# A 4096-cube matmul with GELU: two groups of output blocks pass from one level of Strassen to two, and the first group is planned anew

## The chip, the core and the metric

The kernel runs on one core of a Trainium2 chip. The metric is the device time of one execution in microseconds (us). The profile names the engines PE (TensorE, matmuls), PEld (its weight loads), DVE (VectorE), ACT (ScalarE), POOL (GpSimd) and SP (SyncE). POOL and SP do no arithmetic here: each issues DMAs, in the order in which they stand in its own queue, and sixteen DMA engines carry them out. The kernel before takes 1444.3 us in the median of three runs (1443.88 to 1444.35).

## The reference

```python
m, k, n = 4096, 4096, 4096            # a: m x k, b: k x n, both float32
x = np.matmul(a, b)
out = 0.5 * x * (1 + np.tanh(np.sqrt(2 / np.pi) * (x + 0.044715 * x**3)))   # float32
```

## The kernel before

**Blocks.** A, B and the output are each cut into four quadrants of 2048 x 2048. Rows of A are taken in four rows of blocks (mb 0 to 3; each has 512 rows of the upper and 512 of the lower half), columns of B in four blocks (nb 0 to 3; 512 columns of the left and 512 of the right half). One row of A against one block of B is a *group*: 16 groups, each 1024 x 1024 of the output over the whole inner size 4096. Plainly done, a group is 512 matmuls of 128 x 128 weights by 512 columns.

**One level of Strassen.** In Winograd's form a group is seven products P1 to P7 of sums of quadrants, 64 matmuls each: 448. Operands are float16. B is cast from float32 on its way in (a POOL DMA); A is cast in the same way into a staging buffer and turned by DVE (STREAM_TRANSPOSE). DVE makes the sums of quadrants (`combine2`, L956).

**Three kinds of group.** The list `groups` (mb, nb) orders them: row 0 takes B's blocks 0 1 2 3, row 1 takes 3 0 1 2, row 2 takes 2 3 0 1, row 3 takes 1 2 3 0.

- Group 0 (`first_group`, L782) is written out by hand: the first half of the inner size plainly (L633), the second half by Strassen (L589), 480 matmuls, so that work can start before all quadrants are there.
- Groups 1 to 5 are *raw groups* (`raw_group`, L1502): quadrants of B are loaded, their sums made in place and used at once (L589), and those sums that later groups need are stored to DRAM as *units* (`k_unit`, 512 KB each, by SP). Some of their products are cut once more (`RAW_CUT`): one cut product is 110 matmuls of 256 columns (L1041) and two of 512 in place of 64.
- Groups 6 to 15 are taken in pairs (`late_pair`, L1765): two blocks of B stand side by side for one row of A, and each of P1 to P7 is done by a second level of Strassen, in fourteen steps (`ORDER`) of 8 matmuls of 512 columns (L1864): 112 a product, 784 a pair. Units come back from DRAM (POOL), or B's quadrants are cast again from the input, for the units named in `FROM_INPUT`; `cast_unit` casts from DRAM to DRAM, so that a later pair can fetch. Sums between the four accumulators of each half are moved by ACT copies (L1873, L1876) and DVE adds (L1314, L1319).

`PARK` names pairs that put eight partial sums in DRAM and read them again. When a row of A ends, `turn_quad` loads the next row's four quadrants. Each block's squares (`square`, ACT) and each row's (`weigh`) are summed, for a check of the numbers' range at the end.

**What sets the order.** From group 1 on nothing is issued when it is written: each step is put in a `Plan` with its dependencies, and `schedule` (L235) orders each engine's queue by due times and by tables of costs (`COST`, `MOVE`, `WEIGHT`); `CHOICE` and `EARLIER` are hand-set exceptions. The result is a fixed order on each engine; on the chip only semaphores decide when each step starts.

## Time and profile before

| | us |
|---|---|
| median of the runs (3) | 1444.3 |
| the profiled execution: span from first to last instruction | 1444.0 |
| PE busy | 1434.2 |
| DVE busy | 1224.2 |
| ACT busy | 706.2 |
| groups 4 and 5 (matmuls of the two raw groups) | from 402.0 to 591.3 |
| the five pairs | from 591.3 to 1438.2 |

The span is the time of one core from its first to its last instruction. A busy engine has an instruction running; the DMA issues of POOL and SP are not counted. The share of the DMA engines adds up the time of packets, which overlap: it goes over 1 (1.34 where nothing but casts runs), so it does not by itself say how much more the engines could carry. The granted TensorE clock is 1.00 throughout.

### The profile page before, as it was taken

What the parts mean: (1) busy time and instruction counts of PE and PEld (TensorE: products, weight loads), DVE (VectorE), ACT (ScalarE), POOL (GpSimd) and SP (SyncE); (2) the same over time, 40 slices, a digit from 0 to 9 for tenths busy, and PEclk for the clock granted to TensorE, in tenths of its full rate; (3) what the DMA queues carried; (4) which work ended last, traced back from release to release, by engine and by line L of the source; (5) the groups of instructions that cost most, each with busy time, mean ns of one, the idle gap of its engine ahead of it and who ended that gap; (6) DMA issues with size and microseconds to landing.
All of it is one profiled execution on the core that took longest, in us unless ns stands there. A gap on an engine that the chain in (4) does not pass through costs nothing.

```text
span 1444.0 us, 20205 instructions
## 1 busy us (share of the span) xinstructions
PE 1434.2 (99%) x7011; PEld 686.1 (48%) x7011; DVE 1224.2 (85%) x1335; ACT 706.2 (49%) x1484; POOL 484.8 (34%) x888
## 2 busy tenths in 40 slices
PE   9999999999999999999999999999999999999998
PEld 3444464564545646444444444444444444444443
DVE  2598988996879999989998999888997998968776
ACT  5656764465885453463645413462564612433133
POOL 8765251343244513332322343221323212211120
PEclk9999999999999999999999999999999999999999
DMA  9999999999999999998979999979899966875773
GB/s 170 198 221 240 299 268 267 258 269 263 241 240 244 242 307 248 269 299 280 315 268 324 260 326 316 315 228 322 235 342 248 323 225 226 301 253 209 264 255 119
DMA packets 205181, 378.94 MB, mean 262 GB/s; under 512 B 21008, under 2 KB 115728, under 8 KB 205072
## 3 DMA queue, kind: packets, MB, share of 16 engines
q0 software_dynamic: 146752, 245.42, 70.5%
q1 hardware_dynamic: 58320, 132.15, 24.3%
q8 instruction: 57, 0.93, 0.2%
q14 instruction: 52, 0.43, 0.1%
HBM read 333.45 MB, written 138.42 MB: 327 GB/s over the span
## 4 chain that ended last, share of the span: by engine, by line
PE 93%; DMA 3%; POOL 1%; DVE 1%; issue 1%; ACT 0%; DVEq 0%; ACTq 0%; POOLq 0%
PE acc L1864 56%; PE acc L589 29%; PE acc L1041 6%; PE acc L633 2%; DMA stage<-in_a_dram 2%; DMA out_dram<-y 1%; POOL bR L493 1%; POOL stage L493 1%; DMA bR<-k_unit 1%; DMA bR<-in_b_dram 0%; DVE bR L956 0%; DVE stage L956 0%; ACT y L1292 0%; DVE y L1314 0%; DVE acc L1319 0%
## 5 line engine op out<-in xcount | busy, mean ns | idle before, releaser
L1864 PE MATMUL acc<-bR 128*128 128x512 f16 x1536 | 339.5, 379 | 0.1
L956 DVE TENSOR_TENSOR bR<-bR 128x2048 f16<-128x2048 f16 (+1 forms) x163 | 268.0, 1658 | 41.0 <-PE acc L1864 27.7
L1864 PEld LDWEIGHTS <-bR 128*128 128x128 f16 x1776 | 173.8, 98 | 209.9 <-issue 0.4
L830 POOL DMA_DIRECT2D bR<-k_unit x234 | 126.6, 543 | 434.0 <-PE acc L1864 318.0
L589 PE MATMUL acc<-bR,aT 128*128 128x512 f16 x1024 | 226.2, 379 | 0.0
L1864 PE MATMUL acc<-bR,aT 128*128 128x512 f16 x1008 | 223.6, 379 | 0.0
L830 POOL DMA_DIRECT2D bR<-in_b_dram x256 | 138.0, 545 | 221.2 <-DVE bR L956 69.3
L1864 PEld LDWEIGHTS <-aT 128*128 128x128 f16 x1344 | 131.5, 98 | 158.6
L1876 ACT COPY acc<-acc 128x512 f32<-128x512 f32 x140 | 79.8, 570 | 227.6 <-PE acc L1864 213.2
L1314 DVE TENSOR_TENSOR y<-acc,y 128x512 f32<-128x512 f32 x253 | 167.0, 682 | 21.3 <-ACT y L1308 9.8
L589 PE MATMUL acc<-bR,aD 128*128 128x512 f16 x832 | 180.9, 379 | 0.0
L589 PEld LDWEIGHTS <-aT 128*128 128x128 f16 x1088 | 106.5, 98 | 123.0
L1394 ACT ACTIVATE y<-bR 128x1024 bf16<-128x1024 f16 x128 | 130.8, 1052 | 55.1 <-DVE y L1399 53.4
L589 PEld LDWEIGHTS <-aD 128*128 128x128 f16 x928 | 90.6, 98 | 110.0 <-DVE aD L574 0.8
L1292 ACT ACTIVATE y<-y 128x512 f32<-128x512 f32 x158 | 97.4, 629 | 87.7 <-DVE y L1314 87.3
L1864 PE MATMUL acc<-bR,aD 128*128 128x512 f16 x624 | 138.4, 379 | 0.3 <-DVE bR L956 0.3
L1864 PEld LDWEIGHTS <-aD 128*128 128x128 f16 x784 | 76.6, 98 | 93.1 <-DVE bR L956 0.8
L1873 ACT COPY y<-acc 128x512 f32<-128x512 f32 x99 | 58.0, 586 | 99.4 <-PE acc L1864 85.9
L1399 DVE TENSOR_TENSOR y<-y 128x1024 bf16<-128x1024 bf16 x120 | 82.0, 685 | 17.4 <-ACT y L1394 16.1
L466 DVE STREAM_TRANSPOSE aT<-stage 128x1024 uint32<-128x1024 uint32 (+2 forms) x42 | 52.5, 1277 | 34.9 <-DMA stage<-in_a_dram 32.1
L1864 PE MATMUL acc<-stage,aT 128*128 128x512 f16 x336 | 75.6, 379 | 0.0
L1319 DVE TENSOR_TENSOR acc<-acc,y 128x512 f32<-128x512 f32 x100 | 67.9, 691 | 4.3 <-ACT y L1873 3.0
(126 smaller groups left out, 1682.0 us busy)
## 6 DMA issues: line engine op xcount, KB each, us to landing
bR<-k_unit POOLq DMA_DIRECT2D x234, 512.0 KB, 7.6
out_dram<-y SPq DMA_DIRECT2D x198, 256.0 KB, 7.2
bR<-in_b_dram POOLq DMA_DIRECT2D x352, 128.0 KB, 6.2
k_unit<-bR SPq DMA_DIRECT2D x76, 512.0 KB, 6.0
stage<-in_a_dram POOLq DMA_DIRECT2D x92, 256.0 KB, 10.1
stage<-k_unit POOLq DMA_DIRECT2D x46, 512.0 KB, 7.8
k_unit<-stage SPq DMA_DIRECT2D x28, 512.0 KB, 5.6
out_dram<-bR SPq DMA_DIRECT2D x46, 256.0 KB, 8.2
```

The source lines that it names most:

```text
L589: nc.tensor.matmul(acc, sa[:, j // 2, i * P : (i + 1) * P, j % 2], sb[:, j, :], start=start and j == 0, stop=stop and j == 3, skip_group_c ...
L830: return plan.add(queue, COST[queue], lambda: eng.dma_start(out=dst, in_=src), r=r, w=w, size=MOVE[what] * SPREAD, weight=weight, **kw)
L956: nc.vector.tensor_tensor(out=dst, in0=xa, in1=ya, op=ALU.add if op > 0 else ALU.subtract)
L1041: nc.tensor.matmul(PS[s][i][:, :] if wide else PS[s][i][:, w * HC : (w + 1) * HC], sa[:, j // 2, r * P : (r + 1) * P, j % 2], rhs(j, wide) ...
L1292: act("gelu", lambda: nc.scalar.activation(t, t, ACT.Gelu_apprx_tanh), [("f", f)], [("f", f)])
L1314: dve("add", lambda: nc.vector.tensor_tensor(out=sm(g), in0=bank(s, i), in1=sm(f), op=ALU.add), [("f", f)], [("f", g), ("p", s, i)])
L1319: dve("add", lambda: nc.vector.tensor_tensor(out=bank(s, i), in0=bank(s, i), in1=sm(f), op=ALU.add), [("f", f)], [("p", s, i)])
L1394: act("square", lambda t=t, src=src: nc.scalar.activation(t, src, ACT.Square), [c(cx)], [("f", f)], slack=60.0)
L1399: dve("add16", lambda t=t, u=u: nc.vector.tensor_tensor(out=u, in0=u, in1=t, op=ALU.add), [("f", f)], [("f", e)], slack=60.0)
L1864: nc.tensor.matmul(bank(w, i), sa[:, jx // 2, r * P : (r + 1) * P, jx % 2], bv[:, jx, :], start=p in "17" and jx == 0, stop=jx == NJ - 1, ...
L1873: act("copy", lambda: nc.scalar.copy(out=sm(f), in_=bank(w, i)), [("p", w, i)], [("f", f)])
L1876: act("copy", lambda: nc.scalar.copy(out=bank(*dst), in_=bank(*x)), [("p", *x)], [("p", *dst)])
```

## The change

Groups 4 and 5 become a sixth pair. Row 0 of A is done by group 0 and three raw groups (1, 2, 3), and rows 1, 2 and 3 wholly by pairs; the order of B's blocks in the rows is now written out (`ROWS`), row 1 beginning with the pair of blocks 1 and 2. The raw groups' extra cuts go with the two groups, so that four of seven remain. Row 1 of A is loaded by `turn_quad` at the end of group 3, and must be there for the first pair. The first pair isn't parked.

Group 0 keeps its 480 matmuls but is written into the plan (after two plain steps). It now also stores block 0's sums P4 to P7 (16 units), which before were stored when block 0 was loaded a second time in group 5; and the squares of three of its quadrants' first halves are taken by DVE, not ACT. Buffers are dealt out differently, the planner's costs, due times and exceptions have new values, and `FROM_INPUT` and `CASTS` name other units.

Over the whole program the instructions that the change removes and adds are these:

| | before | after |
|---|---|---|
| PE: matmuls of 512 columns / of 256 | 6241 / 770 | 6315 / 440 |
| DVE: sums of 128x4096 | 107 | 133 |
| DVE: sums of 2048 columns (all forms) | 402 | 356 |
| DVE: adds of 128x512 | 559 | 591 |
| DVE: adds, sums and squares of 1024 columns | 124 | 132 |
| DVE: turns of 1024 / of 2048 | 57 / 3 | 63 / 0 |
| DVE: adds of 128x256 | 30 | 18 |
| ACT: copies of 128x512 / of 128x256 | 396 / 56 | 440 / 32 |
| ACT: squares of 128x1024 | 128 | 116 |
| POOL: casts of B, 128 KB | 416 | 464 |
| POOL: casts of A, 128 KB / 256 KB | 40 / 108 | 8 / 124 |
| POOL: fetches of a unit, 512 KB | 280 | 304 |
| POOL and SP: parked sums, 256 KB, out and back | 40 and 40 | 32 and 32 |
| SP: stores of a unit, 512 KB | 104 | 98 |

Three places show how the queues change. First PE, where group 3 ends. Before, the last rows of group 3's cut product (L1041) are followed by group 4, the next raw group (L589, acc is the accumulator, bR a buffer of B, aT a turned quadrant of A, aD a sum):

```order
L1041 LDWEIGHTS aD
L1041 MATMUL acc<-bR,aD 128x256
L589 LDWEIGHTS aT
L589 MATMUL acc<-bR,aT 128x512
```

Now the same rows of group 3 (L837) are followed by the first pair (L1653), whose B lies in what was the staging buffer:

```order
L837 LDWEIGHTS aD
L837 MATMUL acc<-bR,aD 128x256
L1653 LDWEIGHTS aT
L1653 MATMUL acc<-stage,aT 128x512
```

So the pairs begin two raw groups earlier in PE's list. Second POOL, which issues the loads for this place. Before, the casts of A's row 1 stand among fetches and the long run of casts for blocks 3, 0 and the units:

```order
L830 DMA bR<-in_b_dram 32x4x512 x146
L830 DMA stage<-in_a_dram 32x8x512 x8
L830 DMA bR<-in_b_dram 32x4x512 x14
L830 DMA stage<-in_a_dram 32x8x512 x8
L830 DMA bR<-k_unit 128x2048 x4
```

Now, with the first pair's P1 and P2 of block 1 cast from the input and block 2's fetched, these loads and A's row 1 stand close together:

```order
L630 DMA bR<-in_b_dram 32x4x512 x5
L630 DMA stage<-k_unit 128x2048
L630 DMA bR<-in_b_dram 32x4x512 x3
L630 DMA stage<-k_unit 128x2048
L630 DMA bR<-in_a_dram 32x8x512 x4
L630 DMA bR<-in_b_dram 32x4x512 x3
L630 DMA bR<-in_a_dram 32x8x512 x4
L630 DMA bR<-in_b_dram 32x4x512 x2
L630 DMA bR<-k_unit 128x2048 x2
L630 DMA bR<-in_b_dram 32x4x512 x8
```

The last row holds the second half of block 1's P2, for the fifth step of the first pair's second product. Third SP, at the start of its queue. Before, it begins with group 0's sixteen outputs:

```order
L696 DMA out_dram<-y 128x512 x12
L696 DMA out_dram<-aD 128x512 x4
L830 DMA k_unit<-bR 128x2048 x3
L830 DMA out_dram<-y 128x512
L830 DMA k_unit<-bR 128x2048
```

Now block 0's stores come ahead of and between them:

```order
L630 DMA k_unit<-bR 128x2048 x2
L630 DMA k_unit<-aD 128x2048 x2
L630 DMA k_unit<-bR 128x2048 x2
L630 DMA out_dram<-y 128x512
L630 DMA k_unit<-bR 128x2048 x4
L630 DMA out_dram<-y 128x512 x10
```

Ten stores of 512 KB thus stand ahead of all but one of group 0's outputs.

The diff, cut to its core (new names with a trailing underscore are helpers of the new `first_group`):

```diff
-BUSY = {"PE": 13.0, "DVE": 15.5, "ACT": 18.0, "POOL": 10.4, "SP": 15.5}
+BUSY = {"PE": 20.2, "DVE": 15.3, "ACT": 20.4, "POOL": 12.2, "SP": 5.0}
...
-N_RAW = 6
+CHOICE = {}
+EARLIER = {}
+N_RAW = 4
 RAW_MAKES = {}
-RAW_CUT = {1: "P3", 2: "P7 P3", 3: "P3", 4: "P7 P3", 5: "P7"}
+RAW_CUT = {1: "P3", 2: "P7 P3", 3: "P3"}
 GROUPS = {
+    4: modes_of(m="P1 P2 P3 P4 P5 P6 P7"),
+    5: modes_of(m="P1 P2 P3 P4 P5 P6 P7"),
...
+SQ = {"12": True, "11": True, "22": False, "21": True}
+ROWS = ((0, 1, 2, 3), (1, 2, 3, 0), (3, 0, 1, 2), (3, 2, 1, 0))
...
-FROM_INPUT = ((0, "P2"), (1, "P1"), (1, "P2"), (1, "P3"), (2, "P3"), (3, "P3"))
+FROM_INPUT = ((0, 'P1'), (0, 'P2'), (0, 'P3'), (1, 'P3'), (1, 'P1'), (1, 'P2'), (3, 'P3'))
+STORE_AT = {}
...
-CASTS = {4: ((1, 'P3'), (2, 'P3')), (8, 'P5'): ((0, 'P2'),)}
+CASTS = {(8, 'P5'): ((1, 'P3'), (1, 'P1')), (4, 'P5'): ((0, 'P3'),), (4, 'P6'): ((0, 'P1'),), (4, 'P2'): ((0, 'P2'),)}
...
-PARK = (6, 8, 10, 12, 14)
+PARK = (8, 10, 12, 14)
...
-CHANGED_A = (2, 3)
-CHANGED_B = {(nb, name) for nb, pairs in ((0, (10, 14)), (2, (6, 8, 12))) for name in NAMES
+CHANGED_A = (1, 2, 3)
+CHANGED_B = {(nb, name) for nb, pairs in ((0, (4, 10, 14)), (2, (6, 8, 12))) for name in NAMES
...
+    def first_group():
+        X, Y = 0, 1
...
+        load_b_("11", 0)
+        load_a_("21", 0)
+        plain_pe("11", "11", "11", X, True)
+        square(b_slot["12"], 0, "12", range(4), SQ["12"])
+        square(b_slot["11"], 0, "11", range(4), SQ["11"])
+        load_a_("12", 0)
+        load_b_("22", 0)
...
+        gate = load_a_("12", 1)[-1:]
...
+        keep_t("P7", S["12"][lo], (0, 1), gate, EARLY_STORE)
+        for i in half_pe(X, lambda q: a_quarter(raw("11"), q), S["11"][hi], True):
+            add_bank(xs[i], X, i)
...
+        first = load_raw(1, "11", slots["b"]["11"])
+        send(3, first[-1:])
...
-        first_group()
-        load_raw(1, "12", slots["b"]["12"])
-        behind[1, "P2"] = load_raw(1, "22", slots["b"]["22"])
-        first_weights()
+        first_steps()
+        ends = first_group()
+        pending = raw_group(1, NAMES, RAW_MAKES.get(1, ()), next_nb=2, ends=ends)
+        pending = raw_group(2, NAMES, RAW_MAKES.get(2, ()), next_nb=3, pending=pending)
+        raw_group(3, NAMES, (), turn=1, pending=pending)
         free_cells.extend(ST)
-        pending = raw_group(1, NAMES, RAW_MAKES.get(1, ()), next_nb=2)
-        pending = raw_group(2, NAMES, RAW_MAKES.get(2, ()), next_nb=3, pending=pending)
-        raw_group(3, ("P1", "P2", "P5"), (), turn=1, pending=pending)
-        free_cells.extend(ST)
-        pending = raw_group(4, ("P3", "P4", "P6", "P7"), RAW_MAKES.get(4, ()), fetch=("P5", "P7"), next_nb=0)
-        raw_group(5, NAMES, RAW_MAKES.get(5, ()), pending=pending)
```

More of the change, by code (lines that the diff above doesn't have):

```diff
@@ L764, in half_path @@
+    before = {}
+    for n, whats in ((0, "A11_0a B12_0a A11_0b B12_0b T11_0a T11_0r T11_0s W11_0"),):
+        for what in whats.split():
+            half = what[-1] == "0" and what != "A11_0"
             if what[0] == "W":
-                xs = range(*(int(x) for x in what[6:].split("-"))) if what[6:] else range(NX)
-                before.setdefault(n, []).append((weigh_first, (what[1:3], int(what[4]), xs)))
+                before.setdefault(n, []).append((weigh_first, (what[1:3], int(what[4]), range(NX))))
@@ L1379, in cast_unit, with spare, square @@
                 dma("POOL", dst, src, [], toks, "raw_b", batch=("cu", nb, name, cc), slack=CAST_SLACK, after=after)
-    def square(slot, nb, quad):
+        on_hand.add((nb, name))
+    def spare(nb):
+        energy["n"] += 1
+        return SPARES[nb][energy["n"] % len(SPARES[nb])]
+    def square(slot, nb, quad, xs=range(8), by_dve=False, lead=0.0):
         half = quad[1]
-        for x in range(8):
+        for x in xs:
             cx = slot * 4 + x // 2
@@ L1657, in p4_ends @@
             if turn:
-                turn_quad(turn, "22", raw("22"), (24, 26))
-            if next_nb is None and gi + 1 in REFETCH:
-                for q in range(QPH):
-                    fetch_unit_to(nb, "P2", q, s21[q])
+                turn_quad(turn, "22", raw("22"), (ST[0], ST[2]))
+            if next_nb is None:
+                free_cells.extend(s21)
         def third():
-            return stages_of(split(Y, blk(s2), made_beside(s22) if turn else here(s22), True), c12)
+            return stages_of(split(Y, blk(s2), here(s22), True), c12)
         later_, after = None, lambda: load_next("22", "22")
@@ L1755, in whole_pair @@
                         fetch_unit_to(nb, name, q, cells[q])
-        for nb in nbs:
-            first_use.difference_update({(nb, name, cc) for cc in range(CH)})
+        on_hand.update((nb, name) for nb in nbs if STORE_AT.get((nb, name)) == ga)
         fetched_by[name] = [o for o in plan.ops[begun:] if o.eng == "POOL"]
```

620 lines of the change are left out of this document (288 added, 332 removed).

## The prediction

> **What bounds the kernel now.** I read the page's busy times and chain first, then what PE waited for, then the chain in order of time, and last the stretches and the DMA queues. The page says that PE is the bound:
>
> ```profile
> PE 1434.2 (99%) x7011; PEld 686.1 (48%) x7011; DVE 1224.2 (85%) x1335; ACT 706.2 (49%) x1484; POOL 484.8 (34%) x888
> PE 93%; DMA 3%; POOL 1%; DVE 1%; issue 1%; ACT 0%; DVEq 0%; ACTq 0%; POOLq 0%
> ```
>
> What PE waited for, all told (us, times, longest):
>
> ```profile
> PE acc L633 <- DVE aT L466: 1.7, 1, 1.7
> PE acc L598 <- DVE table L785: 1.5, 1, 1.5
> PE acc L1864 <- DVE bR L956: 0.3, 1, 0.3
> PE acc L589 <- DVE aD L574: 0.3, 1, 0.3
> ```
>
> Once under way PE loses 0.6 us in the whole run. So work taken from PE is time gained, as long as what feeds it keeps up, and there the cover is thinner: DVE is 85% busy, and the DMA engines carry most of the time. Two views price both sides. The chain in order of time (start, us, what) gives PE's rates and the edges of the groups:
>
> ```profile
> 3.42 4.95 DMA stage<-in_a_dram
> 14.78 26.20 PE acc L633 x120
> 195.37 3.49 PE acc L1041 x32
> 402.02 58.71 PE acc L589 x272
> 591.28 355.71 PE acc L1864 x1648
> ```
>
> A matmul of 512 columns takes 355.71 / 1648 = 0.2158 us, one of 256 columns 3.49 / 32 = 0.1091. Groups 4 and 5 run from 402.02 to 591.28. The first loads move at 3.4 us. The timeline of PE at the start and at the end:
>
> ```profile
> 11.14 1.89 PE L633 MATMUL acc<-bR,aT 128*128 128x512 f16 x8
> 1434.54 3.62 PE L1864 MATMUL acc<-bR,aT 128*128 128x512 f16 x16
> ```
>
> PE does eight real matmuls, stops, and goes on at 14.78 with 8 x 0.2158 = 1.7 us done: from there it runs 14.78 - 1.7 = 13.1 us behind its own work. I call this the lead: a load may be 13.1 us late against PE's count of work before it stops PE again. The last matmul ends at 1438.2, and 5.8 us of last adds and stores follow, which the change leaves.
>
> The stretches (PE, PEld, DVE, ACT, POOL busy, clock, DMA share, GB/s landed), and the DMA queues of three of them in the same order (packets, MB, share):
>
> ```profile
> 10.00:80.00 70.00, 68.25 (x317) 30.61 (x315) 33.10 (x36) 44.35 (x193) 53.79 (x96) 1.00 1.34 198
> 90.00:230.00 140.00, 140.00 (x704) 68.78 (x703) 126.81 (x154) 90.75 (x171) 65.86 (x123) 1.00 1.13 264
> 150.00:156.00 6.00, 6.00 (x30) 2.73 (x28) 6.00 (x7) 3.69 (x11) 0.00 (x0) 1.00 1.04 417
> 591.00:760.00 169.00, 169.00 (x785) 76.62 (x784) 156.80 (x158) 84.96 (x193) 51.33 (x94) 1.00 0.95 286
> ```
>
> ```profile
> q0 software_dynamic: 21628, 13.76, 133.8%
> ...
> q0 software_dynamic: 18360, 16.62, 74.0%
> q1 hardware_dynamic: 7846, 20.21, 38.6%
> ...
> q1 hardware_dynamic: 884, 2.50, 103.9%
> ```
>
> From 10 to 80 us only casts move: 198 GB/s, so 128 KB (131,072 bytes) cost 0.662 us of all sixteen engines. From 150 to 156 only stores move: 417 GB/s, so 512 KB cost 1.257 us and a 256 KB output 0.629. From 90 to 230 both are mixed, and these prices explain 16.62 MB / 198 + 20.21 MB / 417 = 83.9 + 48.5 = 132.4 of 140 us, or 0.946, pauses in it counted as loss. So the engines are all but full there already. The granted clock is 1.00 in every row, and nothing here changes it.
>
> **The change part by part.** *PE.* The two raw groups take 591.28 - 402.02 = 189.3 us; the pair in their place is 784 x 0.2158 = 169.2. By counts it is the same: 330 matmuls of 256 columns go, 74 of 512 come, 16.0 - 36.0 = -20.0 us. Group 0 keeps its 480 matmuls. **-20.0 us**, all on the path.
>
> *DVE, ACT, POOL.* Prices by form (busy, mean ns), with one row of ACT and one of POOL behind them:
>
> ```profile
> L1314 DVE TENSOR_TENSOR y<-acc,y 128x512 f32<-128x512 f32 x253 | 167.0, 682 | 21.3 <-ACT y L1308 9.8 <-PE acc L1864 6.8 <-PE acc L1041 2.0
> L956 DVE TENSOR_TENSOR bR<-bR 128x4096 f16<-128x4096 f16 x67 | 153.0, 2287 | 33.0 <-PE acc L1864 27.7 <-DMA bR<-k_unit 5.1
> L956 DVE TENSOR_TENSOR bR<-bR 128x2048 f16<-128x2048 f16 x96 | 115.1, 1218 | 8.0 <-PE acc L589 5.7 <-DMA bR<-in_b_dram 0.9 <-PE acc L1041 0.7
> L1399 DVE TENSOR_TENSOR y<-y 128x1024 bf16<-128x1024 bf16 x120 | 82.0, 685 | 17.4 <-ACT y L1394 16.1
> L466 DVE STREAM_TRANSPOSE aT<-stage 128x1024 uint32<-128x1024 uint32 x37 | 44.2, 1225 | 29.4 <-DMA stage<-in_a_dram 26.5 <-ACT y L607 1.5 <-ACT stage L502 1.3
> ...
> L1876 ACT COPY acc<-acc 128x512 f32<-128x512 f32 x140 | 79.8, 570 | 227.6 <-PE acc L1864 213.2 <-DVE y L1314 14.0
> ...
> L830 POOL DMA_DIRECT2D bR<-in_b_dram x256 | 138.0, 545 | 221.2 <-DVE bR L956 69.3 <-DMA bR<-in_b_dram 41.9 <-PE acc L589 41.3
> ```
>
> 26 x 2.287 - 46 x 1.218 + 32 x 0.682 + 8 x 0.685 + 6 x 1.225 less three long turns of 2.3 and twelve short adds of 0.4 gives 59.5 - 56.0 + 21.8 + 5.5 + 7.4 - 11.7 = +26 us: 1250 of some 1424, 88% for 85%. A pair already runs with DVE at 156.80 / 169 = 93% and PE does not wait, so I cost it at **0**; the cover is that DVE works ahead, and the rival below prices its end. *ACT*: 44 copies more at 0.57, 24 short ones and 12 squares fewer, +4 us at 49% busy: 0. *POOL*: 48 more issues of 0.55 us at 34% busy: 0 for itself; what its queue holds up is the next term, since a cast that waits for a buffer stops all behind it. *Tail*: the last pair is as before, 0.
>
> *The DMA engines up to the first pair.* This is the step that matters: the pair comes 189 us earlier, and its operands with it. Count the queues down to the last row of the POOL piece shown above, the second half of block 1's P2. POOL has by then 288 casts of B of 128 KB, and of A 8 of 128 KB and 60 of 256 KB: 288 + 8 + 120 = 416 units of 128 KB, 416 x 0.662 = 275.4 us. Six fetches, at the store's price: 7.5. SP has by then the 84 stores of blocks 0 to 3 (105.6) and the 64 outputs of row 0 (40.3), whose buffers the pair takes over. The sum is **428.8 us**. Moving from 3.4 us on without a pause it is done at 432.2. PE's work before that step is 480 + 1096 matmuls of 512 and 440 of 256 for group 0 and three raw groups, and 112 + 32 of the pair: 1720 x 0.2158 + 440 x 0.1091 = 419.2 us; with the lead of 13.1 it stands there at 432.3. So with perfect engines the load lands just as PE comes, and each per cent that they lose after the casts of the first 80 us (76.6 us of the 428.8) costs PE 3.5 us. At the mixed stretch's 0.946 the other 352.2 take 372.3, and the stall is 20 us; at 1.00 it is 0. The truth lies between: 0.946 holds pauses in which the queues of before had nothing to send, while the queues now are never empty so early. I take the middle, 0.973: 362.0, a stall of 9.8, and with a us from landing to use **+11 us** (0 to 21). Two earlier places are as tight: at the first sum of A's second half, 104 units of 128 KB at 68.8 + 3.4, a turn (1.2) and a sum (1.2) meet PE at 62.2 + 13.1 with 0.7 us to spare, and at group 1's third quarter 192 units, 15 stores and 18 outputs (157.3 us) leave 3 us before PE, at 152.0. Each can stop PE for a us; I put **+1**.
>
> Over the run the DMA engines get 48 more casts (31.8 us), 24 more fetches (30.2), and lose 6 stores and 16 moves of parked sums (17.6): +44 us, most of it early. After the first pair the later pairs have the load that the row of 591 to 760 shows, 169 us in which PE lost nothing.
>
> **The sum**, against the profiled execution's 1444.0: 1444.0 - 20.0 + 11 + 1 = **1436 us**. The median of the runs is 0.3 above that execution, which I leave out.
>
> A rule weighed against these rows: the Trainium skill, DMA: Bandwidth & Descriptors, section Bandwidth, has the memory's side bind transfers between HBM and SBUF at about 358 GB/s for a core. The casts' row speaks against it, since 198 GB/s landed in float16 are 396 read in float32. What the rule would make of the pinch is the last rival.
>
> **The rivals.** *The engines keep up.* Backlogged queues lose next to nothing, and PE meets each load as it lands: 1424 to 1428. For it: the casts' 70 us, without a pause. Against it: the mixed row's 0.946. *The mixed stream loses more.* Casts wait in POOL's queue for buffers that DVE and PE free, and the stall reaches 17 to 23 us in all (no change) at 0.959 to 0.944, and more below that: at 0.92 it is 32, and the time 1456. From 0.944 down this is slower than before; the row of 90 to 230 stands at that edge. *DVE becomes the bound.* It was idle for 1444.0 - 1224.2 = 219.8 us; if it can shed none of that, the span is 1250 + 220 = 1470, and it is slower unless 23 us of it go. Part is forced, as where it waits for PE's accumulators:
>
> ```profile
> DVE bR L956 <- PE acc L1864: 67.6, 69, 2.9
> DVE aT L466 <- DMA stage<-in_a_dram: 32.1, 10, 9.2
> ```
>
> Against it: the first are a us each, and the longest of the second, 9.2 us, is in the first loads, where DVE now has squares to do. *A ceiling on bytes.* If what is read and written in memory counted, the 416 casts read 109 MB, and fetches, stores and outputs are 64 MB more; were these held to the 382 GB/s that the row of 90 to 230 shows by the same count (2 x 16.62 + 20.21 MB in 140 us), 173 MB end at 456, a stall of 24 and the two us of above, and 1450. By the page's 358 they would take 483 us, and the time be some 1478; the casts' row excludes that figure, not the mechanism. *That the change doesn't do what it says* is excluded by the counts of PE's list.
>
> **How the numbers follow.** Changes under 0.2% (2.9 us) can't be told from none here. My forecast, a stall of 4 to 17 us (1428 to 1441), has 0.48; the engines keeping up 0.18; the mixed stream losing more 0.21, of which 0.10 falls within 0.2%; DVE 0.09 (0.03 within); the ceiling 0.04 (slower). So faster 0.66, same 0.13, slower 0.21. The range leaves out half of the second case and the worst of the last three: 1426 to 1455; the likeliest case's own is 1428 to 1441.
>
> **What would show it.** Right: PE's matmuls busy some 20 us less; its waits name DMA loads of bR, some 10 us, in the steps of the first pair near 400 to 435 us, and nearly none after; stretches up to there have the DMA engines full at 260 GB/s or more. Wrong: waits of PE on DVE's sums spread over the pairs (DVE), waits already in group 0 or in groups 1 to 3 (mixed stream), or no wait at all.

## The result and the profile after

The changed kernel takes **1477.2 us** (median; 1474.5 to 1479.7) against 1444.3: a ratio of **1.0229** (95% interval 1.021 to 1.0248), slower by 33 us. The prediction was 1436, range 1426 to 1455. The profiled execution has a span of 1475.6 us, 31.6 above the one of before.

The page after, its busy line and its chain:

```profile
PE 1426.0 (97%) x6755; PEld 661.7 (45%) x6755; DVE 1260.0 (85%) x1346; ACT 716.9 (49%) x1492; POOL 512.1 (35%) x936
...
PE 42%; DVE 0%; ACT 0%; issue 0%
```

PE has 256 matmuls fewer, as counted, but is busy only 8.2 us less, not 20.0, and idle for 1475.6 - 1426.0 = 49.6 us where it was idle for 9.8. The chain reaches back 42% of the span on PE alone, then breaks up. So, between the two profiled executions: -20.0 of work, +11.8 of matmuls that run slower, +39.8 of idle time, together 31.6.

The view of PE's waits (us, times, longest) names DVE's sums first, but it only says who came last:

```profile
PE acc L1653 <- DVE bR L756: 11.3, 7, 4.8
PE acc L537 <- DVE stage L756: 10.6, 3, 7.0
PE acc L537 <- DVE aD L756: 5.1, 1, 5.1
```

The stretches after (PE, PEld, DVE, ACT, POOL busy, granted clock, DMA share, GB/s):

```profile
10.00:100.00 90.00, 80.34 (x361) 35.22 (x360) 68.42 (x87) 78.33 (x267) 54.19 (x95) 0.98 1.30 208
100.00:190.00 90.00, 81.33 (x364) 36.09 (x363) 71.50 (x86) 51.61 (x82) 34.53 (x64) 0.96 1.10 281
190.00:300.00 110.00, 109.19 (x574) 56.01 (x573) 90.67 (x106) 54.26 (x76) 36.03 (x67) 1.00 1.01 273
300.00:400.00 100.00, 93.81 (x522) 51.08 (x520) 83.18 (x103) 67.12 (x105) 39.51 (x73) 0.98 1.14 276
400.00:560.00 160.00, 156.33 (x773) 74.97 (x772) 150.25 (x159) 86.52 (x191) 82.39 (x151) 1.00 1.13 269
560.00:720.00 160.00, 149.52 (x685) 67.18 (x683) 134.57 (x127) 62.16 (x128) 39.52 (x72) 0.99 0.87 259
720.00:860.00 140.00, 136.61 (x630) 61.13 (x629) 128.45 (x124) 75.11 (x172) 40.04 (x73) 1.00 0.94 294
860.00:1440.00 580.00, 580.00 (x2689) 262.99 (x2688) 506.45 (x527) 226.57 (x450) 178.18 (x327) 1.00 0.88 272
```

and before, the first of them:

```profile
10.00:100.00 90.00, 87.97 (x408) 39.34 (x406) 51.90 (x57) 56.66 (x224) 66.64 (x119) 1.00 1.32 202
```

Length less PE's busy time gives the idle time by stretch: 9.7 us up to 100 (2.0 before), 19.3 from 100 to 560, 13.9 from 560 to 860, and none from there to 1440. The loss has three places, and the last 580 us run as before. PE's longer pauses in its timeline (start, us, instructions; in brackets the pause ahead and what ended it):

```profile
66.15 5.34 PE L1920 MATMUL acc<-bR,aT 128*128 128x512 f16 x24 [0.95 <-DVE y L1114]
83.53 8.67 PE L537 MATMUL acc<-aD 128*128 128x512 f16 x32 [5.12 <-DVE aD L756]
...
184.07 9.58 PE L537 MATMUL acc<-stage,aD 128*128 128x512 f16 x32 [7.05 <-DVE stage L756]
...
376.92 15.65 PE L537 MATMUL acc<-stage,aD 128*128 128x512 f16 x64 [3.06 <-DVE stage L756]
...
467.85 3.41 PE L1653 MATMUL acc<-bR,aT 128*128 128x512 f16 x15 [1.41 <-DMA bR<-in_b_dram]
548.19 7.08 PE L1653 MATMUL acc<-bR 128*128 128x512 f16 x32 [0.67 <-DVE bR L756]
615.34 8.75 PE L1653 MATMUL acc<-bR,aT 128*128 128x512 f16 x32 [4.82 <-DVE bR L756]
668.59 7.07 PE L1653 MATMUL acc<-bR,aD 128*128 128x512 f16 x32 [3.06 <-DVE bR L756]
719.70 7.07 PE L1653 MATMUL acc<-bR,aD 128*128 128x512 f16 x32 [2.60 <-DMA bR<-in_b_dram]
```

They show part of the 11.8 us of slower matmuls too. Thirty-two matmuls take 7.07 us at 668.59; behind the pauses at 83.5, 184 and 615 they take 8.67, 9.58 and 8.75, and the 64 at 377 take 15.65 for 13.98: together 7.5 us more. The stretches of ten us there (PE busy, clock, DMA share, GB/s) show why:

```profile
80.00:90.00 10.00, 6.47 (x23) 0.83 1.31 217
...
180.00:190.00 10.00, 5.93 (x16) 0.66 1.06 375
```

The granted clock is lowered as these pauses end (it is 0.50 from 184 to 187 us): 0.83 over ten us is 3.4 us at half speed, 0.66 is 6.8. Most of the other 4.3 us seems to be the breaks themselves. The last matmul of a row is shown to end 0.16 us after the next could begin (24 matmuls have 5.34 us for 24 x 0.2158 = 5.18), which adds to the busy time only where PE then stops. PE stops 31 times here and 5 times before, and 26 x 0.16 makes 4 us. That is worked out, not tried.

### The profile page after: what moved, and what is told of

It is laid out like the page before. It is cut to its first block, busy times and chain, and to the rows that moved or that the text cites. A ratio compares the mean times of both kernels' runs of the same rounds, so it can differ in the third digit from the quotient of the medians.

```text
span 1475.6 us, 19759 instructions
## 1 busy us (share of the span) xinstructions
PE 1426.0 (97%) x6755; PEld 661.7 (45%) x6755; DVE 1260.0 (85%) x1346; ACT 716.9 (49%) x1492; POOL 512.1 (35%) x936
## 5 line engine op out<-in xcount | busy, mean ns | idle before, releaser
L1653 PE MATMUL acc<-bR 128*128 128x512 f16 x1280 | 285.0, 379 | 1.0 <-DVE bR L756 1.0
L1653 PE MATMUL acc<-bR,aT 128*128 128x512 f16 x1168 | 260.1, 381 | 8.1 <-DVE bR L756 6.6
L1653 PEld LDWEIGHTS <-bR 128*128 128x128 f16 x1744 | 170.3, 98 | 207.7 <-DVE bR L756 2.3
L1653 PEld LDWEIGHTS <-aT 128*128 128x128 f16 x1664 | 163.0, 98 | 207.6 <-issue 10.4
L756 DVE TENSOR_TENSOR bR<-bR 128x4096 f16<-128x4096 f16 (+1 forms) x114 | 211.0, 1857 | 24.8 <-PE acc L1653 16.9
L630 POOL DMA_DIRECT2D bR<-in_b_dram x288 | 156.1, 545 | 204.6 <-DMA bR<-in_b_dram 64.9
L1114 DVE TENSOR_TENSOR y<-acc,y 128x512 f32<-128x512 f32 x283 | 187.1, 685 | 32.0 <-PE acc L1653 25.8
L1653 PE MATMUL acc<-bR,aD 128*128 128x512 f16 x816 | 180.8, 379 | 5.8 <-DVE bR L756 3.1
L1653 PEld LDWEIGHTS <-aD 128*128 128x128 f16 x1024 | 100.1, 98 | 127.1 <-issue 6.6
L537 PE MATMUL acc<-bR,aT 128*128 128x512 f16 x544 | 120.8, 379 | 3.5 <-ACT acc L1304 1.4
L1653 PE MATMUL acc<-stage,aT 128*128 128x512 f16 x496 | 111.6, 379 | 0.9 <-DVE aT L756 0.9
L1653 PE MATMUL acc<-stage,bR 128*128 128x512 f16 x464 | 104.9, 379 | 0.0
L1200 ACT ACTIVATE y<-bR 128x1024 bf16<-128x1024 f16 x83 | 83.6, 1050 | 40.9 <-DVE y L1205 36.6
L537 PE MATMUL acc<-stage,aD 128*128 128x512 f16 x384 | 88.0, 392 | 10.6 <-DVE stage L756 10.6
L1205 DVE TENSOR_TENSOR y<-y 128x1024 bf16<-128x1024 bf16 x102 | 70.1, 688 | 29.7 <-ACT y L1200 28.4
```

The lines of the kernel that those rows point to most:

```text
L537: nc.tensor.matmul(acc, sa[:, j // 2, i * P : (i + 1) * P, j % 2], sb[:, j, :], start=start and j == 0, stop=stop and j == 3, skip_group_c ...
L630: return plan.add(queue, COST[queue], lambda: eng.dma_start(out=dst, in_=src), r=r, w=w, size=MOVE[what] * SPREAD, weight=weight, **kw)
L756: nc.vector.tensor_tensor(out=dst, in0=xa, in1=ya, op=ALU.add if op > 0 else ALU.subtract)
L1114: dve("add", lambda: nc.vector.tensor_tensor(out=sm(g), in0=bank(s, i), in1=sm(f), op=ALU.add), [("f", f)], [("f", g), ("p", s, i)])
L1200: act("square", lambda t=t, src=src: nc.scalar.activation(t, src, ACT.Square), [c(cx)], [("f", f)], slack=60.0, lead=lead)
L1205: dve("add16", lambda t=t, u=u: nc.vector.tensor_tensor(out=u, in0=u, in1=t, op=ALU.add), [("f", f)], [("f", e)], slack=60.0, lead=lead)
```

## The experiments

All times are medians beside runs of the kernel before on the same chip, which stayed at 1443.6 to 1444.6. Kernels of the changed kind scatter more: single runs lie mostly within 4 us of their median, at most 8, so that differences below 3 us are not read and one of 4 us is weak. Most edits also make the planner lay out anew what follows them.

### One suspect at a time in groups 0 and 1

What ends the pauses at 83.5 and 184 us? ACT, the stores and DVE were suspects. First ACT: group 0's squares of A's rows, written over the staged rows again.

```diff
-act("weigh0", lambda r=r: weigh_first(quad, cc, (r,), junk), toks, [("w0",)],
+act("weigh0", lambda r=r: weigh_first(quad, cc, (r,)), [], [*toks, ("w0",)],
```

> The changed kernel with one thing undone: in group 0 the squares of A's rows are written over the staged rows, as before, and not into one common scratch tile. Theory (ACT holds the staging buffers in group 0: 112 of these ACTIVATEs come every 0.54 us in the changed kernel and came every 0.40 before, 112 x 0.14 = 16 us of ACT): they come every 0.40 again, ACT's busy time from 60 to 100 us falls from 38.3 of 40 to 32 or less, PE's pause at 83.5 us (5.1) and the one at 184 (7.1) at least halve, and the time falls by 6 to 16 us, to 1461 to 1471. Rival (DVE's own queue or the stores make these pauses): the spacing falls, the pauses stay within a us of 5.1 and 7.1, and the time stays within 3 us of 1477.

Measured: 1483.7 us, 1.0285 (1.0255 to 1.0315): slower by 6.5, which neither theory had. An ACT row and PE's two pauses:

```profile
66.04 0.40 ACT L477 ACTIVATE aD<-aD 128x256 f16<-128x256 f16 x1
```

```profile
83.90 9.97 PE L537 MATMUL acc<-aD 128*128 128x512 f16 x32 [6.77 <-DVE aD L756]
181.92 8.32 PE L537 MATMUL acc<-stage,aD 128*128 128x512 f16 x30 [5.17 <-DVE stage L756]
```

The squares come 0.40 us apart again (the one ahead starts at 65.64), ACT's busy time from 60 to 100 us falls from 38.3 to 29.7, and the pauses stay. ACT's spacing alone is not the cause. The loss stands mostly later, as at 324.71 (a pause of 4.49 us for 1.24) and at 451.07 (3.89, new). In place, a square also waits for the turn of its rows, and the planner lays out all that follows anew; which of the two costs the 6.5 us is open.

Then the stores of block 0's sums.

```diff
-dma("POOL", cell(x), unit(nb, name)[:, q, :], [("u", nb, name, q)], [c(x)], "unit")
+dma("POOL", cell(x), unit(nb or 2, name)[:, q, :], [("u", nb or 2, name, q)], [c(x)], "unit")
...
-for q, x in zip(qs, cells):
-    store_unit(0, name, q, x, after, slack=slack)
+return
```

> The changed kernel without the 16 stores of block 0's sums (P4 to P7, 512 KB each; the later fetches of block 0's sums take as many bytes from block 2's, so the output of that block is not the product). Theory (the stores of 512 KB that go out from 100 to 195 us keep buffers and DMA engines from the loads): the pause of PE at 184 us (7.1 us, behind a sum that waits for a store of the buffer it overwrites) shrinks below 2 us, its drop of the granted clock goes, and the time falls by 8 to 14 us, to 1463 to 1469; the pause at 83.5 stays. Rival (the loads or DVE are late in themselves): the pause at 184 stays at 4 us or more and the time falls by less than 4 us.

Measured: 1473.5 us, 1.0204 (1.0182 to 1.0226), 3.8 less, which the scatter hardly tells from nothing. PE's pauses of a us and more from 70 to 430 us, and one later:

```profile
83.07 10.04 PE L537 MATMUL acc<-aD 128*128 128x512 f16 x32 [4.45 <-DVE aD L756]
103.09 8.57 PE L537 MATMUL acc<-bR,aT 128*128 128x512 f16 x32 [3.07 <-ACT acc L2033]
365.80 8.63 PE L537 MATMUL acc<-stage,aD 128*128 128x512 f16 x32 [2.71 <-DVE stage L756]
...
407.54 1.03 PE L837 MATMUL acc<-bR,aD 128*128 128x256 f16 x8 [1.89 <-ACT acc L851]
424.64 1.91 PE L837 MATMUL acc<-bR,aD 128*128 128x256 f16 x16 [1.99 <-DVE bR L756]
...
712.23 7.07 PE L1653 MATMUL acc<-bR,aD 128*128 128x512 f16 x32 [3.51 <-DVE bR L756]
```

The pause at 184 is gone altogether, so these stores had a part in it. In the changed kernel DVE's sum there waits for a store of the buffer that it overwrites, and POOL's casts for another:

```profile
182.79 1.23 DVE L756 TENSOR_TENSOR stage<-bR,stage 128x2048 f16<-128x2048 f16 x1 [3.60 <-DMA k_unit<-bR]
```

```profile
182.63 4.27 POOL L630 DMA_DIRECT2D stage<-in_b_dram  x8 [14.54 <-DMA k_unit<-stage]
```

But of 7 us and a drop of the clock only 3.8 stay saved. At 103 us ACT's copy ends later, and PE waits 3.07 us for 1.13. To the steps at 408 and 425 PE comes some 10 us earlier and waits there, and its four pauses from 606 to 766 us make 14.5 us where those from 615 to 772 made 11.6. The theory was right on the cause, and wrong on what its removal is worth.

Then DVE, in two steps: most squares of block 0 left out, and all but a few of all blocks.

```diff
-square(b_slot["12"], 0, "12", range(4), SQ["12"])
-square(b_slot["11"], 0, "11", range(4), SQ["11"])
+square(b_slot["12"], 0, "12", range(1), False)
+square(b_slot["11"], 0, "11", range(1), False)
...
-square(b_slot["22"], 0, "22", range(4, 8))
-square(b_slot["21"], 0, "21", range(4, 8))
```

> The changed kernel without most of the squares of block 0 of B (1 of 8 pieces for each of the two halves is squared, on ACT; 23 DVE squares, 30 DVE adds and 7 ACT squares are left out, so that the check of B's sizes sees a part of block 0 alone): DVE has 23 x 0.66 + 30 x 0.69 = 36 us less to do before 200 us. Theory (DVE is the engine that is late in groups 0 and 1): the pauses at 83.5 and 184 us both go or fall below 2 us, and with the clock's drops behind them the time falls by 12 to 20 us, to 1457 to 1465. Rival (ACT or the stores): at least one of the two stays above 4 us and the time falls by less than 8 us. The pauses at 377, 615, 669 and 720 us should stay in either case, since nothing there is changed.

The total, 5289 us, can't be compared: with squares of part of block 0 alone the program's own bounds on B's sizes don't hold, and its second path runs behind the first. The first path's profile can be read. PE, and DVE ahead of its pause:

```profile
81.87 8.32 PE L537 MATMUL acc<-aD 128*128 128x512 f16 x27 [4.55 <-DVE aD L756]
...
182.87 7.33 PE L537 MATMUL acc<-stage,aD 128*128 128x512 f16 x27 [6.21 <-DVE stage L756]
```

```profile
70.02 2.37 DVE L449 STREAM_TRANSPOSE aT<-aD 128x1024 uint32<-128x1024 uint32 x2 [5.71 <-DMA aD<-in_a_dram]
```

Both pauses stand, and ahead of the first DVE itself is idle for 5.7 us, waiting for a load of A. Now the squares of all blocks (the bounds are opened too):

```diff
-        for x in xs:
+        for x in list(xs)[:1] if (nb, half) not in energy else ():
...
```

> The changed kernel without the check of B's sizes (one piece of each half of a block is squared, the other pieces are left out, and the bounds are opened so that the check passes): before 400 us DVE has 23 squares of 0.66 and 4 x 30 adds of 0.69 less, 98 us, and ACT some 97 squares of 1.05. Theory (DVE's load makes the pauses in groups 0 to 3, where it is 90% busy): the pauses at 83.5, 184 and 377 us, 15 us together, shrink to under 5, the drops of the clock behind them go, and the time falls by 12 to 25 us, to 1452 to 1465. Rival (the order in which loads, sums and stores stand makes them, and DVE waits in it itself): DVE is idle 80 us more before 400, two of the three pauses stay above 3 us, and the time is within 6 us of 1477 either way.

Measured: 1483.3 us, 1.027 (1.025 to 1.0289), 6 us slower with 79 us of DVE's busy time gone (1180.7 for 1260.0; the 98 added up durations that overlap). From 10 to 400 us DVE is busy for 254 us where it was busy for 314. The pauses at 81 and 180 are 3.6 and 6.8; the one at 377 is gone, and PE, which comes earlier to the first pair, waits there instead:

```profile
435.27 6.11 PE L1653 MATMUL acc<-bR,aT 128*128 128x512 f16 x15 [5.63 <-DMA bR<-in_b_dram]
449.47 5.83 PE L1653 MATMUL acc<-bR 128*128 128x512 f16 x15 [4.65 <-DVE bR L756]
```

So DVE isn't the bound in groups 0 to 3, though the waits name it. The first of these rows is a load of block 1 for the first pair, at about the time that the prediction named, but not the load that it named: it stands 33 matmuls into the pair, and the named step 112 further on. In the changed kernel the named step is the row at 467.85: its load comes some 36 us later than the 432.2 worked out for perfect engines, and PE comes so late itself that it waits only 1.41 us.

### What the lowered clock costs

Ahead of the six steps that wait longest stand matmuls that add zero.

```diff
+FILL = {328: 24, 705: 32, 1520: 14, 2240: 22, 2386: 14, 2561: 12}
...
+for _ in range(k):
+    nc.tensor.matmul(bank(s, i), idle[:, :], cell(x)[:, :NC], start=False, stop=True, skip_group_check=True)
+real()
```

> The changed kernel with PE's six longest pauses filled: ahead of the step that waits at 83.5, 184, 377, 615, 669 and 720 us stand 24, 32, 14, 22, 14 and 12 matmuls that add zero times something to the step's own accumulator (118 x 0.2158 = 25.5 us, as long as the six pauses together; the sums are unchanged, and no other instruction or order is). Theory (a pause of some 3 us or more is answered with a granted clock of 0.5 for 3.4 us or a multiple, 17.1 us in all, and this costs time of its own): no drop of the clock is left before the end, and the time falls by 5 to 9 us (half of 17.1, less what of it lies within the pauses), to 1468 to 1472. Rival (the slow stretches cost nothing in the end, since what feeds PE is late anyway and the next step would wait longer): the drops go and the time stays within 3 us of 1477.

Measured: 1491.5 us, 1.0324 (1.0307 to 1.0341): 14 us slower, and the total answers another question. At 615 and 669 us the filling reads a buffer that the awaited sum rewrites, so it stood behind the pause: 36 matmuls, 7.8 us, added. The other four stood ahead of their steps. The first two, and the place at 615 with the step before it:

```profile
84.86 7.08 PE L537 MATMUL acc<-aD 128*128 128x512 f16 x32 [0.76 <-DVE aD L767]
...
183.62 7.07 PE L537 MATMUL acc<-stage,aD 128*128 128x512 f16 x32
...
545.50 7.08 PE L1664 MATMUL acc<-bR 128*128 128x512 f16 x32 [0.67 <-DVE bR L767]
615.49 6.59 PE L626 MATMUL acc<-bR,idle 128*128 128x512 f16 x22 [7.65 <-DVE bR L767]
```

In the first two rows the 32 matmuls take 7.07 us, the clock stays at 1.00 up to 600 us, and at the step that began at 548.19 PE is 2.7 us ahead. At 615 it waits 7.65 us for 4.82, and starts at 615.5 for 615.3: the whole gain is gone. So a lowered clock costs PE time, but here PE spends what it gains in waiting for the same sum. Theory and rival each held for one half.

### The emptied tables, and the order of the blocks

The diff empties the planner's two tables of exceptions. The kernel before without its own:

```diff
-CHOICE = {
-    14: 4, 29: 2, 42: 3, 50: 1, 59: 3, 71: 2, 73: 2, 75: 1, 77: 1, 78: 2, 83: 1, 84: 1,
-    85: 2, 86: 1, 90: 3,
-}
-EARLIER = {
-    2407: 12,
-}
+CHOICE = {}
+EARLIER = {}
```

> The kernel before with its two tables of exceptions emptied (15 choices of buffers and one instruction moved up), which the changed kernel has empty too; the work is the same to the instruction. Theory (the changed kernel loses time in its first pairs because its order and its buffers are the rules' own, without exceptions): PE, which lost 0.6 us before, now pauses in the first pairs after 591 us for 5 to 16 us in all, with drops of the granted clock behind the longer pauses, and the time is 1449 to 1464. Rival (the pauses of the changed kernel come from its more work alone): within 3 us of 1444.

Measured: 1460.6 us, 1.0122 (1.0103 to 1.0142): 16.6 us lost with the same work, as much as half of what the change loses in all. Its tables had served the whole run: of the idle time without them 4.3 us lie from 100 to 560 us and 7.4 from 560 to 860. The two longest of PE's waits, where before it lost 0.6 us once under way:

```profile
PE acc L1859 <- DMA stage<-k_unit: 3.0, 2, 2.2
PE acc L584 <- DVE bR L951: 2.5, 1, 2.5
```

Then the other way round: the changed kernel with tables of its own, for the part behind 560 us.

```diff
-CHOICE = {}
-EARLIER = {}
+CHOICE = {44: 4, 54: 2, 59: 4, 68: 3, 71: 1}
+EARLIER = {2278: -6, 2411: 50, 2552: 25, 2565: 25, 2714: 25, 2836: 50, 2874: 12}
```

> The changed kernel with its two tables of exceptions filled again: 5 choices of buffers and 7 instructions moved, found for the stretch behind 560 us alone; the work is the same to the instruction. Theory (the pauses at 615, 669 and 720 us come of the buffers and the order that the rules choose without exceptions, as the kernel before loses 16.6 us without its tables): at least two of the three pauses go, with 7 to 10 us and the drop of the clock at 616, and the time falls by 8 to 16 us, to 1461 to 1469. Rival (the work of the second pair, its loads or DVE's sums, is too much for the time whatever the order): pauses of as much stand elsewhere between 560 and 800 us, and the time falls by less than 4 us.

Measured: 1466.5 us, 1.0171 (1.014 to 1.0202), 10.7 us less than the changed kernel. The pauses at 615 and 669 are gone, and the longest left from 560 us on is

```profile
732.12 7.24 PE L1653 MATMUL acc<-bR,aT 128*128 128x512 f16 x32 [1.63 <-DVE bR L756]
```

PE's idle time from 560 to 860 us is 5.4 us for 13.9 (in the profiled execution, the fastest of four). So the second pair had room for its work; what it lacked was a better dealing of buffers and a better order. In the changed kernel POOL fetches at 603.92, when PE lets a buffer go, DVE sums at 613.00 what has landed, and PE starts at 615.34: PE waits for a chain that begins with its own step 11 us before.

Last the order of the blocks in row 1, put back (`FROM_INPUT` and `CASTS` stay as the new order has them):

```diff
-ROWS = ((0, 1, 2, 3), (1, 2, 3, 0), (3, 0, 1, 2), (3, 2, 1, 0))
+ROWS = ((0, 1, 2, 3), (3, 0, 1, 2), (3, 0, 1, 2), (3, 2, 1, 0))
```

> The changed kernel with one of its parts undone: row two of A takes B's blocks in the old order, four and one first, then two and three. Theory (the first pair's operands are the tight place, and beginning at blocks two and three is what makes them come in time, since their sums are stored earlier and block one's are not stored): the first pair waits for loads of 10 us or more in one pause or two between 400 and 500 us, where the changed kernel waited 2.8 us, and the time rises by 10 to 30 us, to 1487 to 1507. Rival (which blocks come first makes no difference, or the new order itself makes the pauses at 615, 669 and 720): these three pauses go, and the time falls by 5 to 13 us, to 1464 to 1472.

Measured: 1500.3 us, 1.039 (1.0373 to 1.0408), 23 us slower, as the theory had it:

```profile
452.37 9.86 PE L1653 MATMUL acc<-bR,aT 128*128 128x512 f16 x32 [16.77 <-DMA bR<-in_a_dram]
490.07 9.80 PE L1653 MATMUL acc<-bR,aT 128*128 128x512 f16 x32 [10.56 <-DVE bR L756]
```

Beginning this row at blocks 1 and 2 is thus not what costs; with the old order the first pair's operands stop PE for 27 us.

### The DMA engines up to 560 us

The 64 stores of the first row's outputs, 40 us of these engines' work, are dropped and nothing else.

```diff
 def store_out(gi, i, ih, jh, f, after=()):
+    if gi < 4:
+        plan.add("SP", COST["SP"], lambda: None, r=[("f", f)], size=0.001, after=after)
+        ...
+        return
```

> The changed kernel without the 64 stores of the first row's outputs (groups 0 to 3, 256 KB each, before 440 us; this quarter of the output is not written): 64 x 0.629 = 40 us of work less for the DMA engines, and nothing less for any other engine. Theory (up to 560 us the DMA engines are the bound: they show a share over 1.08 and 255 to 305 GB/s in each stretch up to there, and 24 stores and casts too many keep loads late, so that PE's pauses between 170 and 470 us, 18 us in all, are theirs): these pauses go but for 5 us, the pause at 83.5 and those at 615, 669 and 720 stay, and with the clock's drops the time falls by 12 to 22 us, to 1455 to 1465. Rival (order or buffers make them; the engines have room): the pauses between 170 and 470 stay above 10 us, and the time falls by less than 5.

Measured: 1461.4 us, 1.011 (1.0093 to 1.0126): 15.8 us less, in the theory's range. The stretches from 100 us on:

```profile
100.00:190.00 90.00, 89.15 (x414) 40.32 (x413) 79.67 (x95) 59.47 (x94) 38.58 (x72) 1.00 1.10 275
...
300.00:400.00 100.00, 96.90 (x527) 50.91 (x525) 88.59 (x106) 79.80 (x141) 40.96 (x75) 1.00 1.07 238
400.00:560.00 160.00, 158.49 (x779) 75.70 (x777) 147.52 (x154) 74.86 (x158) 76.50 (x139) 1.00 1.03 256
```

PE's idle time from 100 to 560 falls from 19.3 to 5.5 us (none from 190 to 300), with the clock at 1.00. The pauses of 5 us at 84 and 597 stay. DVE, whose sums the waits name, has the same to do. The pause at 184 goes here too, with block 0's stores in place: it took both kinds of stores to make it. A store left out also gives its buffer back at once, but in the changed kernel the only engine that waits for an output's store from 100 to 560 us is ACT, for 2.4 us in all. So the DMA engines' work is the likely cause; that it is their time, and not the bytes that the memory moves, isn't shown, since a store left out takes away both.

> Both edits at once: the tables filled, and the 64 stores of the first row's outputs left out. Theory (two separate causes, DMA engines that are full up to 560 us and an unordered second pair behind it): the two gains add up, the pauses left are the one at 83.5 us and some 6 us of short ones, and the time falls by 22 to 36 us, to 1441 to 1455. Rival (what one saves the other pays, since PE that comes earlier waits longer in the next tight place, as it did at 615 us where it came 2.7 us earlier after the filled pauses): the sum falls short of the two single gains by 8 us or more.

Measured: 1454.8 us, 1.0064 (1.0047 to 1.008): 22.4 us less, where the two single gains make 26.5. They mostly add up; 4 us are paid elsewhere, as at 497 us, where PE waits 3.9 us for a fetch.

### Group 0: two limits, one behind the other

One load of A less, 5.3 us of the DMA engines, ahead of the pause at 83.5.

```diff
+if (quad, cc) == ("11", 1):
+    got = [plan.add("POOL", COST["POOL"], lambda: None, w=toks, size=0.001, batch=("a0", quad, cc), slack=400.0)
+           for _ in load_a(quad, cc)]
+else:
     got = [dma("POOL", dst, src, [], toks, "raw_a0", batch=("a0", quad, cc), slack=400.0, lead=lead)
```

> The changed kernel without one load of group 0: the second half of A's quadrant 11 (four casts of 256 KB, 8 x 0.662 = 5.3 us of work for the DMA engines) is not loaded, and its turn and its squares run on what the staging buffer held before, so that DVE, ACT and PE have the same to do (the output of the first row is not the product). Theory (the pause at 83.5 us is the casts': from 3 to 100 us they run without a gap at some 206 GB/s, and the operands of that step are the last of them): the pause shrinks to 1 us or less and the drop of the clock behind it goes, so that PE is 4 to 8 us ahead at 150 us; what stands later is laid out anew by the rules and may take it back. Rival (the turns, sums and squares between the load and the step make it): the pause stays at 3.5 us or more, as it did with DVE's squares away and with the stores away.

Measured: 1483.1 us, 1.0269 (1.025 to 1.0289), 5.9 slower. PE, and ACT ahead of PE's second pause:

```profile
79.99 7.08 PE L537 MATMUL acc<-aD 128*128 128x512 f16 x32 [1.52 <-DVE aD L756]
...
100.66 3.57 PE L537 MATMUL acc<-bR,aT 128*128 128x512 f16 x8 [6.66 <-ACT acc L2038]
```

```profile
97.99 0.42 ACT L477 ACTIVATE stat_b<-stage 128x256 f16<-128x256 f16 x1
98.53 0.42 ACT L477 ACTIVATE stat_b<-stage 128x256 f16<-128x256 f16 x1
```

The pause at 83.5 was the loads': it falls to 1.5 us and the clock stays up behind it. But the next place takes more than that back: ACT's copies into PE's accumulators stand in its queue behind rows' squares, one every 0.54 us.

> Three edits at once: that load of group 0 left out, the 64 stores of the first row's outputs left out, the tables filled. Against the kernel with the last two alone (1454.8) it differs in the load only. Theory (three separate causes, of 5 to 8, 16 and 11 us): no pause over 2 us is left before 480 us, and the time is 4 to 9 us below 1454.8, 1446 to 1451, which leaves 2 to 7 us of the 33 without a name. Rival (what is saved at 83.5 is paid in the next tight place): the pause goes, others grow by as much before 560 us, and the time is within 2.5 us of 1454.8.

Measured: 1462.2 us, 1.0118 (1.0091 to 1.0146): 7.4 above the pair of edits, with the same pause (6.66 us at 100.6). Neither expectation had that. The last two runs take ACT's squares of A's rows away, with and without the load, on top of the filled tables and the dropped outputs (the bounds are opened here too).

```diff
-act("weigh0", lambda r=r: weigh_first(quad, cc, (r,), junk), toks, [("w0",)],
+plan.add("ACT", 0.01, lambda: None, r=toks, w=[("w0",)], batch=("w0", quad, cc), slack=FIRST_SLACK, every=0.01)
...
```

> Tables filled, the 64 outputs of the first row left out, and the squares of A's rows in group 0 left out (112 ACTIVATEs with their reads, some 60 us of ACT before 110 us; the check's sums for these rows are a constant and its bounds open); all loads stand. It differs in these squares alone from the kernel that took 1454.8. Theory (the casts are the first limit in group 0 and ACT the one behind it): the pause at 83.8 us stays above 3.5 us, and the time is within 2.5 us of 1454.8. Rival (ACT is the limit): the pause falls below 1.5 us and the time by 5 us or more.

> As the run before, and also without the load of the second half of A's quadrant 11: tables filled, outputs of the first row, one load and the rows' squares of group 0 left out. It differs from the kernel that took 1462.2 (with a pause of 6.7 us at 100.6) in the rows' squares alone. Theory (loads first, ACT behind them): no pause over 2 us is left before 300 us, none of the clock's drops either, and the time is 1443 to 1452, 3 to 12 us below the kernel without the squares alone. Rival (the gain is taken back in the next tight place, DVE or the loads of group 1): the pauses at 83.5 and 100.6 go and others grow, and the time stays at 1453 or more.

Measured: 1458.4 (1.0104; 1.0087 to 1.0121) with the load, and **1448.8** (1.0034; 1.0022 to 1.0047) without it. With the load, PE at its first tight step and, without the load, the first row past it and the one long pause that is left:

```profile
85.42 9.17 PE L537 MATMUL acc<-aD 128*128 128x512 f16 x32 [8.25 <-DVE aD L756]
```

```profile
92.53 2.15 PE L537 MATMUL acc<-bR,aT 128*128 128x512 f16 x8 [0.99 <-DVE bR L756]
...
494.25 6.59 PE L1658 MATMUL acc<-bR,aD 128*128 128x512 f16 x16 [4.14 <-DMA bR<-k_unit]
```

Without the squares alone the pause at 85 us stays (8.25 us; the time is 3.6 above 1454.8, a us more than expected, at the edge of the scatter). Without both, no pause from 30 to 300 us is over 1 us. So loads are the first limit there and ACT the second, and either relief by itself is worth nothing.

The four edits together take away 28.4 of the 33 us. Three of them leave work out, so they show where the time goes and not how to win it back. What is left is 4 us above the kernel before although it does less work, and no version here that does the whole of it beats that kernel. No run has the sixth pair without the new group 0, or the new group 0 without the pair, so the loss isn't divided between these two parts of the change.

## Why the prediction was wrong

**PE, -20.0.** Right in its count. The profile shows 6755 matmuls for 7011.

**"The granted clock is 1.00 in every row, and nothing here changes it."** This step failed, and it was no term at all. Every pause that the change made of 3 us or more but one brought a lowered clock, 7.5 us in the rows shown. The Trainium skill, TensorE: Matmul & The Clock Gate, section What's actually happening, says that an idle window of some 3.4 us halves the clock, and that this window runs freely; its section Why this matters for your kernels advises no gap over about 3 us. The half speed and the 3.4 us agree with this trace (0.50 from 184 to 187 us, 0.83 over 80 to 90, which is 3.4 us at half); how long a pause must be is less sharp here, see the end.

**The later pairs: "169 us in which PE lost nothing".** This step failed. I let a row of before stand for the pairs of after. That row showed a plan with exceptions fitted to it, and the diff empties the tables; I costed nothing for that. The run without tables lost 16.6 us in the kernel before, and the run with new tables won 10.7 in the kernel after: of the 13.9 us of idle time from 560 to 860 it took away 8.5.

**The DMA engines up to the first pair, +11.** The work was counted rightly, its rate was not. From 80 us to the landing of the named load at 467.85 POOL's queue moved 44.38 MB, 3.66 of them fetches, and SP's 59.10. By the prediction's own prices that is 40.72 MB / 198 + 62.76 MB / 417 = 356 us of work (352.2 were forecast) in 388 us: 0.92, and not 0.973. "The queues now are never empty so early" is the step that failed. In most stretches of 20 us the same prices give 0.93 to 0.98, as in the forecast; the loss stands in 100 to 120 us (0.77), 200 to 220 (0.79) and 260 to 300 (0.77), where too little was under way. How much of that is PE's own lateness, which lets buffers go late, is open. For 0.92 the prediction itself had a stall of 32 us; PE stood at the named step at 467.85 and not at 432.3, some 36 us late, but it paid at 83.5, 184 and 377 us and not at 400 to 435, since loads and stores ahead of the named load came late too. In the words of the prediction it is the case of waits "in groups 1 to 3 (mixed stream)", to which it gave 0.21. The ceiling on bytes gave some 1478 in one of its cases; that the measured time is near is luck, since in the prediction's count, with casts twice, the memory moved 372 GB/s from 80 to 468 us, and the time has other causes. A higher ceiling isn't excluded.

**"Each can stop PE for a us; I put +1."** This step failed by size. The two places were the right ones: the first sum of A's second half cost 5.1 us at 83.5 and group 1's, as near as the trace tells it, 7.05 at 184, and both lowered the clock. With 0.7 and 3 us to spare on a count that took the engines as perfect, the likeliest value was not one us.

**DVE, +26 us at 0, and ACT, +4 us at 0.** DVE's zero was right: 79 us of its work less won nothing, so the rival in which DVE becomes the bound falls. ACT's zero was right only because loads stopped PE first. The rows' squares, which the new scratch tile spaces by 0.54 us for 0.40, were in the diff and not costed; they came to light as a pause of 6.66 us once one load was gone. Without them that pause goes; whether the wider spacing alone makes it, or their place in ACT's queue, was not tried.

**The tail at 0** held: from 860 us on PE has no pause, and 5.3 us follow its last matmul for 5.8 before. POOL's issues as such held too; what its queue held up is in the term of the DMA engines.

## What to carry over

Before a row of the old profile stands for work that a change lays out anew, ask what in the old layout was fitted by hand: emptying the tables of exceptions cost the kernel before 16.6 us, half as much as this whole change lost. Where several feeders run within a few per cent of the engine that bounds the kernel, take two away together before calling either innocent: in group 0 the load alone and the squares alone won nothing, and both won 6 us (1454.8 to 1448.8). The engine that a wait names is the last of a chain, so look at what that engine waited for, and add to a pause of 3 us or more the slow matmuls behind it.

## What the runs showed of the hardware

The clock's drop has no single threshold of the pause. In the run without stores a pause of 2.71 us at 365.80 was followed by 32 matmuls in 8.63 us, so the clock was lowered; after 3.51 us at 712.23 of the same execution they took 7.07, and it wasn't. In the traces of all sixteen kernels, from 30 to 1400 us, none of the 17 pauses of 1.5 to 2.04 us was followed by a lowered clock, all 44 of 3.62 us or more were, and of the 28 pauses between 13 were (two of them one matmul apart), among them four of the eight that lasted 3.06 us.

An ACTIVATE that adds up its row, with its read of the sum, comes every 0.54 us where all of them write one scratch tile, and every 0.40 where each writes over its own input, with 0.42 and 0.40 us of its own busy time (the rows shown of the run with a load less, and of the run in place). What holds the next one back is not shown.
